# Gated linear attention in a hybrid trunk: the projections of a pair of heads traced ahead of the mixing of the pair before

## The chip, the cores and the metric

The kernel runs on one core of one Trainium2 chip. A core has a matrix engine (TensorE, PE in the profile, with its weight loads shown as PEld), VectorE (DVE), ScalarE (ACT), GpSimd (POOL), and SyncE (SP), which here only issues DMAs. The engines run side by side; each takes its own instructions strictly in the order in which the program lists them, and they wait for one another through semaphores. The metric is the device time of the program in microseconds: the median of several runs. One further execution is taken with the profiler; the views quoted below come from that execution.

## The reference, cut to what matters

One layer of a decoder trunk on 512 tokens and 16 meta tokens, 2048 wide. The normalised input goes through one wide projection, whose columns feed three causal mixers on separate heads: a gated DeltaNet (6 heads), gated linear attention or GLA (5 heads) and a forgetting attention (5 heads). All are multiplied by SiLU gates and go through one output projection. The change is in GLA alone:

```python
def gla_chunked(q, k, v, log_g):
    """S_t = diag(alpha_t) S_{t-1} + k_t v_t^T ; o_t = q_t S_t.
    q, k, log_g [B,H,T,dk]; v [B,H,T,dv]. Returns [B,T,H,dv]."""
    ...
        attn = jnp.einsum('bhid,bhjd,bhijd->bhij', q_c, k_c, dec)
        o = jnp.einsum('bhid,bhdv->bhiv', qd, s) + jnp.einsum('bhij,bhjv->bhiv', attn, v_c)
        s = s * gl[..., :, None] + jnp.einsum('bhjd,bhjv->bhdv', kd, v_c)

    log_g = jax.nn.log_sigmoid(gl @ w_gk2.astype(f32) + b_gk.astype(f32)) / GLA_NORMALIZER
    o_gla = gla_chunked(to_heads(gq, GLA_HEADS) * GLA_DK ** -0.5, to_heads(gk, GLA_HEADS),
                        to_heads(gv, GLA_HEADS), to_heads(log_g, GLA_HEADS))
    o_gla = gated_head_norm(o_gla, gz, gla_norm_w.astype(f32))
```

## The kernel before, in words

**Stages.** The program works through: loading and splitting the input, the gates, DeltaNet in two groups of three heads (keys, values, queries, inverse, mixing), the SiLU gates of GLA, GLA itself, five forgetting heads, and the output projection. All of the input projection is done in blocks of 128 columns by one helper, `inproj` (line 188): each block loads its weights in two halves of 128 x 1024 through SP (L136), splits each half into a high and a low part (ACT at L144, DVE at L145), and issues matmuls at L174: for each of 16 slices of the inner dimension three products (high by high, high by low, low by high), in one part of 512 columns (48 matmuls) or in two of 264 (96 matmuls, where the meta tokens are needed as well). The results stay in PSUM tiles of tag "b" (four buffers) until DVE takes them out, scaled (L285 and L287, helper `evac`).

**GLA.** The five heads go in pairs, p = 0, 1, 2 (the last pair is a single head). For each pair, one function does two things. The first is *projection*: keys gk and queries gq (for the last pair one block holds both), one block of values gv for each head, transposed on PE into token order (`tok_values`, L640 and L643, with copies by ACT at L641 and L644), and the gates: a small matmul (L669, tile pgk), bias (L671), a log-sigmoid on DVE and ACT (L672 to L675), and a running sum (L676), which gives gc. The second is *mixing*, from line 677 on: score matmuls at L717 (tiles pss) in eight levels, for blocks of 64, 32, 16, 8, 4, 2, 1 and the diagonal. For each level DVE and ACT prepare scaled keys and queries (L695 to L703) in two shared sets of tiles (kq), and DVE takes the scores out, by copies (L721, L725) or masked copies (L729). Then come the decayed keys (L736 to L743, with gkd and its transpose pkd), the meta part (L745 to L762), the states (L768, L770), the outputs (L777, L783), the head norm (L789 to L794), a transpose back (L797, tile pgt) and the product with the SiLU gate (L799).

**What sets the order.** The program is not written as one list per engine. A planner takes the instructions with their dependencies and lays out each engine's list when the program is built: of the instructions that it holds to be ready by its own timing, it takes the one with the lowest number of priority. That number counts up by one with each instruction in the order in which the Python code creates them. `tc.high_priority(offset=n)` makes the numbers of the instructions within it lower by n; after the block, the count goes on from where it stood ahead of the block. The split of the weights (lines 142 to 145) uses an offset of 1,000,000, so it is always taken first. Tiles are named by tag, and each tag has a fixed number of buffers: "m" (PSUM, 4) for everything on PE that is not a projection, "b" (PSUM, 4) for projections, "six" (8), "row" (7), "t15" (6), and a few small ones. An instruction that writes a new tile needs a free buffer of its tag.

**Names in the two parts.** Projection: gqk (keys, queries and gc; "six"), gvt (values; "six"), gvm ("t15"), vg, gu and gt ("row"), pvg, pwg and pgk ("m"). Mixing: gdd (tag "gd", 2), a (one buffer, scores of the fine levels), at (shared by all pairs, within the kq tiles), gkd, kdt and gqd ("row"), pss, pkd, pgm, pg0, pgn, pgo and pgt ("m"). Forgetting heads: fqk and fc ("six"), vf ("row"), pvf and others ("m").

Of the kernel before, what the change touches and what calls it, by code (L numbers as in the profile page):

```python
# [77 lines left out]
def tile_hybrid_trunk(ctx, tc, xT, xtok, mtok, w_gate, w_in, w_out, consts, lmask, fin_w, out, dbg=None):  # L78
# [14 lines left out]
    def row(name, dt=F32):  # L93
        return wk.tile([P, 3 + T], dt, tag="row", bufs=7, name=name)

    def t15(name, shape=(P, H, P), dt=F32):
        return wk.tile(list(shape), dt, tag="t15", bufs=6, name=name)
# [547 lines left out]

    kts, qts, ats = [], [], []

    def gla_pair(p):
        R = P if p < 2 else 64
        ne = 2 if p < 2 else 1  # L650
        qk = six.tile([P, 3, T], F32, tag="six", name=f"gqk{p}")
        kT, qT, gc = qk[:R, 0], qk[:R, 1], qk[:R, 2]
# [7 lines left out]
        vt = six.tile([P, 2, S], F32, tag="six", name=f"gvt{p}")  # L660
        vm = t15(f"gvm{p}", (NM, 2, P))
# [12 lines left out]
        A.activation(t, t, AF.Ln, bias=1.0)  # L674
        V.scalar_tensor_tensor(out=u, in0=u, scalar=0.0, in1=t, op0=ALU.min, op1=ALU.subtract)  # L675
        V.tensor_tensor_scan(gc, gsc[:R], u, 0.0, ALU.mult, ALU.add)  # L676
        SC = 1.0 / 16.0
        k4, q4, g4 = (a[:, NM:].rearrange("p (b t) -> p b t", b=NB) for a in (kT, qT, gc))
        n_n = ne * NB
# [4 lines left out]
        def scores(s, li):  # L684
# [11 lines left out]
            if s > 1:  # L696
                V.tensor_tensor(out=dv[:, :, 0, :], in0=ref, in1=gv[:, :, 0, :], op=ALU.subtract)
                A.activation(d, d, AF.Exp, scale=SC)
                V.tensor_tensor(out=kxv[:, :, 0, :], in0=kv[:, :, 0, :], in1=dv[:, :, 0, :], op=ALU.mult)
            else:  # L700
                A.activation(dv[:, :, 1, :], dv[:, :, 1, :], AF.Exp, scale=SC)
                kx = kT[:, NM:]
# [33 lines left out]
        V.tensor_tensor(out=d4, in0=g4[:, :, P - 1 : P].to_broadcast([R, NB, P]), in1=g4, op=ALU.subtract)  # L736
        A.activation(dd, dd, AF.Exp, scale=SC)
        G.tensor_tensor(out=d4, in0=d4, in1=k4, op=ALU.mult)
# [6 lines left out]
        V.tensor_tensor(out=dm, in0=gc[:, NM - 1 : NM].to_broadcast([R, NM]), in1=gc[:, :NM], op=ALU.subtract)  # L745
        A.activation(dm, dm, AF.Exp, scale=SC)
        V.tensor_tensor(out=dm, in0=dm, in1=kT[:, :NM], op=ALU.mult)
# [4 lines left out]
        qd = row(f"gqd{p}")[:, :S][:R]  # L752
        A.activation(qd, gc[:, NM:], AF.Exp, scale=SC)
        G.tensor_tensor(out=qd, in0=qd, in1=qT[:, NM:], op=ALU.mult)
        eg = wk.tile([P, NB], F32, tag="geg", name=f"geg{p}")[:R]
        A.activation(eg, g4[:, :, P - 1], AF.Exp, scale=SC)
        p0 = psm.tile([P, 512], F32, tag="m", name=f"pg0{p}")
# [127 lines left out]
    for g in range(2):  # L885
        for h in range(max(NF, H * g), H * g + H):
            gate_z("dz", h)
        st = dn_keys(g)
# [11 lines left out]
    kts += [kq[0][:, :S], kq[0][:, S : 2 * S]]  # L900
    qts += [kq[0][:, 2 * S :], kq[1][:, :S]]
    ats.append(kq[1][:, S:].rearrange("p (n t) -> p n t", t=P))
    for p in range(3):
        gla_pair(p)
    for h in range(GLA_HEADS):
        dump(f"ogl{h}", zs["gz", h])
    for h in range(FOX_HEADS):
# [176 lines left out]
```

## Time and profile before

| what | us |
|---|---|
| median of 3 runs | 1032.09 |
| lowest and highest run | 1031.01, 1033.81 |
| profiled execution, whole | 1035.39 |
| profiled execution, span from the first to the last instruction | 1033.7 |
| PE busy in the span | 1011.4 |
| weight loads busy (overlap PE) | 910.3 |
| DVE busy | 566.7 |
| ACT busy | 411.7 |
| POOL busy | 136.4 |

The mean granted TensorE clock of the profiled execution is 0.992 of full speed.

How to read the views: a row of a stretch gives its start and end, its length, and for each engine the busy time and the number of instructions, then the granted clock of PE and the share and rate of the DMAs. A row of the timeline gives the start, the duration, the engine, the line, the operation, the tile written and the tiles read (numbers left out), the count of merged instructions, and in brackets the idle time of the engine ahead of it and what ended it. A row of the waits gives who waited for whom, the total, how often, and the longest. Matmuls overlap in the pipeline, so that the duration of one is longer than the distance to the next.

### The profile page before, as it was taken

The page shows a single profiled execution, that of the slowest core. Times are in us where ns is not written, and L with a number is a line of the kernel's source. Part 1 is how long each engine was busy: PE and PEld are TensorE (multiplying, and loading weights), DVE is VectorE, ACT ScalarE, POOL GpSimd, SP SyncE. Part 2 cuts the span into 40 slices and gives each one's busy share as a digit, 9 for nine tenths or more (in the row PEclk, how much of TensorE's full clock was granted, in tenths as well). Part 3 has the DMA queues.
Part 4 walks back from the last instruction along what each step waited for, and adds up shares of the span by engine and source line. Part 5 has one row for each costly group of instructions (what it writes and reads, how often), then busy time and mean ns, then how long its engine had stood idle before and what let it go on. Part 6 is the DMA issues. An engine that isn't in the chain of part 4 may idle for free.

```text
span 1033.7 us, 19032 instructions
## 1 busy us (share of the span) xinstructions
PE 1011.4 (98%) x7799; PEld 910.3 (88%) x7799; DVE 566.7 (55%) x1240; ACT 411.7 (40%) x899; POOL 136.4 (13%) x137
## 2 busy tenths in 40 slices
PE   9999999999999998999989999999999999999996
PEld 7899999989999888899989879898998988888885
DVE  6366868856577883243747474445454574423234
ACT  6644533343455343243444444343333353213223
POOL 0022212221122222100101010110101010000014
PEclk9999999999999998999999999999999999999998
DMA  9613232323222233132112122222232254222244
GB/s 354 239 62 115 83 90 91 102 78 108 78 83 81 78 102 99 49 94 74 62 48 83 44 92 66 91 82 92 82 93 82 93 193 133 82 100 85 102 142 163
DMA packets 42347, 105.15 MB, mean 102 GB/s; under 512 B 10589, under 2 KB 13917, under 8 KB 42260
## 3 DMA queue, kind: packets, MB, share of 16 engines
q1 hardware_dynamic: 28000, 92.33, 26.3%
q10 hardware_dynamic: 14260, 11.61, 4.1%
q8 instruction: 61, 1.00, 0.4%
q14 instruction: 26, 0.21, 0.1%
HBM read 98.74 MB, written 5.05 MB: 100 GB/s over the span
## 4 chain that ended last, share of the span: by engine, by line
PE 66%; DVE 5%; DMA 3%; issue 3%; ACT 2%; POOL 1%; ACTq 0%; POOLq 0%; DVEq 0%
PE pp L174 39%; PE pa L932 15%; DMA sc<-ab 1%; PE pss L717 1%; POOL stgz L294 1%; DVE wlo L145 1%; PE pfo L877 1%; PE pfa L845 1%; PE py L593 1%; PE pb L932 1%; PE pfx L860 1%; DVE ab L465 1%; PE po L608 1%; PE po L607 1%; PE pa L570 0%
## 5 line engine op out<-in xcount | busy, mean ns | idle before, releaser
L174 PE MATMUL pp<-xh,whi 128*128 128x264 f32 (+2 forms) x1456 | 378.2, 311 | 0.8 <-DVE vg L285 0.5
L174 PE MATMUL pp<-xl,whi 128*128 128x264 f32 (+2 forms) x1456 | 378.2, 311 | 0.0
L174 PE MATMUL pp<-xh,wlo 128*128 128x264 f32 (+2 forms) x1456 | 376.5, 310 | 0.0
L174 PEld LDWEIGHTS pp<-xh,whi 128*128 128x128 f32 x1456 | 244.4, 189 | 16.8 <-issue 3.1
L174 PEld LDWEIGHTS pp<-xl,whi 128*128 128x128 f32 x1456 | 245.6, 190 | 14.0 <-issue 1.0
L174 PEld LDWEIGHTS pp<-xh,wlo 128*128 128x128 f32 x1456 | 245.2, 190 | 13.1 <-issue 0.2
L145 DVE TENSOR_TENSOR wlo<-raw,whi 128x1024 fp32r<-128x1024 f32 x110 | 137.1, 1246 | 112.0 <-ACT whi L144 110.4
L144 ACT CAST whi<-raw 128x1024 fp32r<-128x1024 f32 x110 | 115.4, 1049 | 202.3 <-PE pp L174 175.3
L932 PE MATMUL pa<-wloo,oh 128*128 128x512 f32 x224 | 88.0, 393 | 0.0
L932 PE MATMUL pa<-whio,ol 128*128 128x512 f32 x224 | 87.9, 393 | 0.0
L932 PE MATMUL pa<-whio,oh 128*128 128x512 f32 x224 | 78.3, 396 | 0.0
L145 DVE TENSOR_TENSOR wloo<-rawo,whio 128x1024 fp32r<-128x1024 f32 x29 | 35.8, 1236 | 76.4 <-ACT whio L144 76.3
L144 ACT CAST whio<-rawo 128x1024 fp32r<-128x1024 f32 x29 | 30.4, 1049 | 83.8 <-PE pa L932 56.8
L932 PEld LDWEIGHTS pa<-whio,ol 128*128 128x128 f32 x224 | 42.2, 188 | 9.7
L932 PEld LDWEIGHTS pa<-wloo,oh 128*128 128x128 f32 x224 | 42.1, 188 | 9.4
L932 PEld LDWEIGHTS pa<-whio,oh 128*128 128x128 f32 x224 | 41.9, 188 | 9.2
L294 POOL TENSOR_SCALAR stc<-cv 128x528 f32<-128x528 f32 (+1 forms) x18 | 28.1, 1562 | 164.5 <-DVE cv L368 164.5
L368 DVE SCALAR_TENSOR_TENSOR cv<-pb,cpk,cv 128x528 f32<-128x528 f32 (+1 forms) x54 | 40.8, 756 | 0.8
L959 POOL TENSOR_TENSOR acc<-acc,fw 128x512 f32<-128x512 f32 x12 | 15.7, 1348 | 158.6 <-DMA fw<-in_fin_w 158.6
L285 DVE TENSOR_TENSOR pb<-pp,rstd 128x264 f32<-128x264 f32 (+1 forms) x36 | 13.8, 423 | 16.0 <-PE pp L174 15.9
L465 DVE TENSOR_TENSOR ab<-ab,ot 51x30 f32<-51x30 f32 (+14 forms) x60 | 21.4, 357 | 1.4
L463 DVE TENSOR_TENSOR ot<-ab 51x30 f32<-51x30 f32 (+14 forms) x60 | 20.1, 334 | 3.1 <-DMA ab<-scmeta 1.5
(384 smaller groups left out, 1279.8 us busy)
## 6 DMA issues: line engine op xcount, KB each, us to landing
raw<-in_w_in SPq DMA_DIRECT2D x110, 512.0 KB, 3.3
rawo<-in_w_out SPq DMA_DIRECT2D x29, 512.0 KB, 3.3
xt<-in_xtok SPq DMA_DIRECT2D x8, 512.0 KB, 9.9
acc<-in_xtok ACTq DMA_DIRECT2D x16, 256.0 KB, 5.2
out<-acc SPq DMA_DIRECT2D x16, 256.0 KB, 3.0
xs<-in_xT SPq DMA_DIRECT2D x7, 528.0 KB, 6.5
gb<-gd ACTq DMA_DIRECT2D x2, 792.0 KB, 7.4
eg<-gd ACTq DMA_DIRECT2D x8, 192.0 KB, 3.7
```

Source lines behind the costliest of these rows:

```text
L144: A.copy(hi, raw)
L145: V.tensor_tensor(out=lo, in0=raw, in1=hi.bitcast(F32), op=ALU.subtract)
L174: mm = PE.matmul(p_[:, :nt], wt[:, j * m : (j + 1) * m], xx[k][:, t0 : t0 + nt], start=(k == 0 and wt is hi and xx is xh), stop=(k == KT - ...
L285: V.tensor_tensor(out=o, in0=p_[rows], in1=rstd[rows, t0 : t0 + n], op=ALU.mult)
L294: G.tensor_scalar_max(t, src, LOW)
L368: V.scalar_tensor_tensor(out=c, in0=pb[:, t0 + w : w + T], scalar=cwc[:, blk, w : w + 1], in1=c, op0=ALU.mult, op1=ALU.add)
L463: V.tensor_tensor(out=t3, in0=a3[:, j + 1 :, j : j + 1].to_broadcast([NN * 4 + H, m, j]), in1=a3[:, j : j + 1, 0:j].to_broadcast([NN * 4 + ...
L465: V.tensor_tensor(out=a3[:, j + 1 :, 0:j], in0=a3[:, j + 1 :, 0:j], in1=t3, op=ALU.add)
L593: PE.matmul(py[:, j * P : (j + 1) * P], uf[:, b * H + j, :], z[:, j, :], start=True, stop=True)
L607: PE.matmul(pj, at[:, b * H + j, :], y[:, j, :], start=True, stop=False)
L932: PE.matmul(p_, o_[:, s], w_, start=(first and n == 0), stop=(last and n == 2), **kw)
L959: G.tensor_tensor(out=acc[tb, cc], in0=acc[tb, cc], in1=fw[cc], op=ALU.mult)
```

## The change

The function for a pair is cut in two at line 677: `gla_project(p)` holds the projection, the value transposes and the gates, and returns its tiles; `gla_mix(p, st)` holds the rest, unchanged. The calls are then put in another order: projection 0, projection 1, mixing 0, projection 2, mixing 1, mixing 2, where mixings 0 and 1 are created with priority numbers lower by 500. The instructions themselves, their sizes and their tiles are the same.

```diff
@@ -645,7 +645,7 @@
     kts, qts, ats = [], [], []
 
-    def gla_pair(p):
+    def gla_project(p):
         R = P if p < 2 else 64
         ne = 2 if p < 2 else 1
         qk = six.tile([P, 3, T], F32, tag="six", name=f"gqk{p}")
...
         V.tensor_tensor_scan(gc, gsc[:R], u, 0.0, ALU.mult, ALU.add)
+        return R, ne, kT, qT, gc, qk, vt, vm
+
+    def gla_mix(p, st):
+        R, ne, kT, qT, gc, qk, vt, vm = st
         SC = 1.0 / 16.0
...
-    for p in range(3):
-        gla_pair(p)
+    gla = {0: gla_project(0), 1: gla_project(1)}
+    with tc.high_priority(offset=500):
+        gla_mix(0, gla[0])
+    gla[2] = gla_project(2)
+    with tc.high_priority(offset=500):
+        gla_mix(1, gla[1])
+    gla_mix(2, gla[2])
     for h in range(GLA_HEADS):
```

## The prediction

> **What bounds the kernel now.** First the page's busy times, then the same by stretches, to see where TensorE (PE) stands idle; the columns after each stretch are busy microseconds and instruction counts of PE, weight loads, VectorE (DVE), ScalarE (ACT) and GpSimd (POOL).
>
> ```profile
> PE 1011.4 (98%) x7799; PEld 910.3 (88%) x7799; DVE 566.7 (55%) x1240; ACT 411.7 (40%) x899; POOL 136.4 (13%) x137
> ```
>
> ```profile
> 0.00:50.00 50.00, 48.32 (x209) 39.18 (x210) 25.42 (x41) 34.51 (x59) 1.85 (x16) 1.00 0.80 296
> 200.00:250.00 50.00, 47.58 (x521) 45.88 (x521) 30.37 (x58) 18.65 (x31) 9.26 (x10) 0.97 0.30 93
> 400.00:450.00 50.00, 46.98 (x465) 42.80 (x464) 15.61 (x34) 18.27 (x43) 5.33 (x6) 0.93 0.25 76
> 499.00:549.00 50.00, 46.82 (x776) 44.38 (x776) 30.84 (x71) 21.86 (x57) 4.53 (x3) 1.00 0.19 61
> 549.00:558.00 9.00, 9.00 (x67) 7.95 (x66) 4.99 (x7) 2.50 (x4) 0.00 (x0) 1.00 0.24 67
> 558.00:598.00 40.00, 37.59 (x704) 35.55 (x704) 22.79 (x60) 18.17 (x51) 5.04 (x3) 1.00 0.18 62
> 598.00:610.00 12.00, 12.00 (x53) 8.79 (x51) 7.26 (x11) 3.27 (x7) 0.63 (x1) 1.00 0.33 101
> 610.00:646.00 36.00, 35.50 (x428) 31.25 (x427) 22.02 (x50) 15.54 (x37) 5.08 (x3) 1.00 0.20 65
> 646.00:1000.00 354.00, 353.68 (x1921) 304.32 (x1920) 158.71 (x338) 118.90 (x215) 18.82 (x28) 1.00 0.31 103
> 1000.00:1034.00 34.00, 25.40 (x125) 21.09 (x123) 12.60 (x21) 11.45 (x28) 15.69 (x12) 0.91 0.47 157
> ```
>
> PE is idle for 1033.7 − 1011.4 = 22.3 us of the whole span. Most of it lies at the start, in the two DeltaNet inverses (200 to 250, 400 to 450) and in the tail after 1000, none of which the change touches. GLA runs from 499 to 646: 499 to 549 is the mixing of pair 0, 549 to 558 the gates of pair 1, 558 to 598 the mixing of pair 1, 598 to 610 the gates of pair 2, 610 to 646 the mixing of pair 2. PE idles there for 3.18 + 0 + 2.41 + 0 + 0.50 = 6.1 us. That is the most that any order of the same instructions can give back on PE, but for a few tenths hidden in pipelined matmuls. Note the two gate stretches: the mixing stands still in them, and yet PE is busy for 9.00 of 9.00 and 12.00 of 12.00 us, with projections traced later. The waits of PE in and around GLA say what the 6.1 us are:
>
> ```profile
> PE pss L717 <- issue: 3.5, 3, 1.4
> PE pkd L742 <- DVE a L729: 1.1, 1, 1.1
> PE pp L174 <- DVE vg L285: 0.5, 2, 0.3
> PE pg L760 <- ACT gkm L751: 0.5, 1, 0.5
> PE pss L717 <- DVE kq L703: 0.5, 1, 0.5
> ```
>
> "issue" means that nothing in the profile was waited for. All three of these waits cut runs of two score levels (64 short matmuls each) issued back to back, as here:
>
> ```profile
> 520.30 0.76 PE L717 MATMUL pss<-kq 64*32 64x32 f32 x64
> 520.91 0.70 PE L717 MATMUL pss<-kq,kq 64*32 64x32 f32 x59
> 522.96 0.26 PE L717 MATMUL pss<-kq,kq 64*32 64x32 f32 x5 [1.35 <-issue]
> ```
>
> **The change, part by part.**
>
> Work: no instruction, byte or tile is added or removed. The sum is made of order alone: PE's 1011.4 us stay, and only its idle time can move.
>
> The numbers of priority. Counted in the code, a projection of a full pair is 374 instructions, its mixing 346. Before, the order is projection 0 (0 to 374), mixing 0 (374 to 720), projection 1 (from 720). After, projection 1 has 374 to 748, and mixing 0 is traced at 748 but ranks 500 earlier, 248 to 594. So mixing 0 ranks ahead of nearly all of the values and of the gates of pair 1, as before; only gk1, gq1 and the loads and first matmuls of gv2 come to rank ahead of its later levels. Those have run by then anyway (gv2 starts at 491.80, below). Mixing 1 ranks 467 to 813, projection 2 from 748: the same picture. By priority alone hardly anything moves.
>
> What does move is the handing out of tiles. The trace shows that tiles of one tag are given out in the order in which the program creates them, not to whoever is ready:
>
> ```profile
> 508.39 2.93 POOL L738 TENSOR_TENSOR gkd<-gkd,gqk 128x512 f32<-128x512 f32 x1 [30.79 <-ACT gkd L737]
> 527.09 0.63 PE L742 MATMUL pkd<-ident,gkd 128*128 128x128 f32 x4
> 527.56 1.44 DVE L285 TENSOR_TENSOR vg<-pp,rstd 128x264 f32<-128x264 f32 x4
> 549.29 0.71 PE L669 MATMUL pgk<-misc,cpk 16*128 16x264 f32 x2
> 550.04 0.49 DVE L671 TENSOR_SCALAR gu<-pgk,cpk 128x264 f32<-128x264 f32 x1 [0.88 <-PE pgk L669]
> ```
>
> gkd is ready at 508.39 + 2.93 = 511.3, but its transpose into a PSUM tile (tag "m", four buffers) runs at 527.09, behind all scores. The gate matmul pgk of pair 1 needs only misc and a constant, there since long before, and runs at 549.29, when the last "m" tile of mixing 0 has been handed out. After the change the "m" tiles of projection 1 (value transposes, gates) are created before the scores of mixing 0, so these scores must wait for them, whatever their priority.
>
> First scores. They run now at 510.60. The 192 matmuls of gv2 and gv3 start at 491.80, one every 0.12 us:
>
> ```profile
> 491.80 0.28 PE L174 MATMUL pp<-xh,whi 128*128 128x264 f32 x1
> 491.92 0.28 PE L174 MATMUL pp<-xl,whi 128*128 128x264 f32 x1
> 510.60 0.68 PE L717 MATMUL pss<-kq 64*64 64x64 f32 x16
> ```
>
> 192 × 0.12 = 23 us, with some 2 us of other PE work between: done at about 517, transposes and gates by 519. So mixing 0 starts its scores some 9 us later, with the operands of its first two levels long prepared. PE loses nothing: in those 9 us it runs gv3 and then gk2, and gk2 has PSUM, since the values of gv2 are now evacuated at once and not at 527.56.
>
> Gates. Each is a chain on DVE and ACT, for pair 1 from 549.29 to 556.80 + 1.26 = 558.1:
>
> ```profile
> 552.87 0.71 DVE L672 SCALAR_TENSOR_TENSOR gt<-gu 128x528 f32<-128x528 f32 x1
> 556.80 1.26 DVE L676 TENSOR_TENSOR_SCAN gqk<-gsc,gu 128x528 f32<-128x528 bf16 x1
> ```
>
> After the change the gates run under the mixing of the pair before, so the chain of mixings loses about 9 + 12 us of standing still, gives up 9 us at its start, and should end near 625 to 635 and not at 646. On PE this is worth 0, because PE idles 0.00 us in both stretches. What covers it is the stock of projections (gk2, gv4, fk, fv, fq, fz of forget head 0). Were that cover gone, up to 21 us would show. It isn't consumed faster: the shorter GLA needs less of it.
>
> DVE in mixing 0. It gains the gates (two L671 of 0.49, two of 0.71, the scan 1.26: 3.7 us) and the four vg evacuations (1.44 us), 5.1 us in a stretch where it is busy 30.84 of 50. Behind a DVE instruction in the planned order stand the masked copies L729, which free the score tiles, and so PE's next scores. Bounds: 0 (room of 19 us) to 5.1 us (each of them stops PE). I take 1.0, near the lower end: PE's waits for DVE in GLA (0.5 + 1.1 + 0.5) are small beside DVE's 88 us there (the five stretches).
>
> Waits for issue, 3.5 us. Bounds: all go (−3.5) or as many come again (+3.5: pairs of levels in mixing 2, which has none now). With gk2 in stock and DVE slower per level, the levels of mixing 0 should stand more apart; I take one wait of 1.35 away. The wait for kq (0.5) goes too, as those operands are early. The wait of pkd for L729 stays, and what is late next is the same copy.
>
> The Trainium skill ("Runtime: NRT & Kernel Launch", section on instruction fetch) says that crossing an instruction block costs little because the next one is fetched while the current one runs. The issue waits inside unbroken runs of scores, 3.5 us here, do not agree if they are such crossings; by the rule there would be nothing to win there, and the sum below would be −0.5 + 1.0 = +0.5 us.
>
> Switches. PE goes from projections to scores and back at some dozen places; a few more or fewer, at the tenth of a microsecond that a projection needs more than its 0.12 there, is ±0.5; I take 0.
>
> DMAs. The weight loads on SP keep their order. The one DMA of GLA on ACT's queue (the query rows of pair 2) is issued some 15 us earlier, inside mixing 0, where ACT is busy 21.86 of 50; what stands behind it is ACT's exponentials. Between 0 and a few tenths; 0 taken.
>
> Sum: −1.35 − 0.5 + 1.0 = −0.9, about −1 us. The profiled execution took 1035.4 us, 1.7 more than its span of 1033.7 and 3.3 more than the median of the runs, 1032.1. It would take 1034.4, the runs 1031.1.
>
> **The rivals.**
>
> Likeliest, PE-bound as before: the chain of mixings gets shorter, PE doesn't notice. For it: 353.68 of 354 us busy after 646, and the two gate stretches full. 1031.1, by itself between 1029 and 1034.
>
> The change does nothing at all: rank and hand-out undo each other, and even the chain keeps its length. Then 1032.1. Against it speaks pgk, which is held by tiles alone. It falls within the same class of result.
>
> Faster: the stock of projections between the levels grows so much that PE's waits in mixings 0 and 1 go: 3.5 + 1.1 + 0.5 + 0.5 = 5.6, so 1026.5. For it: projections wait for evacuated values (vg, 0.5), and after the change these are evacuated earlier. Against it: pairs of levels come from DVE's order in one mixing, which is kept.
>
> A part of the faster side, at 2 in 100: GLA is bounded by its chain, not by PE, and the 21 us come off: 1011. It needs a PE that could have done more in 549 to 558.
>
> The Trainium skill ("Perfetto Trace Analysis", section on the most-contended engine) says that matmul busy time flatters and weight-load busy time should be read. Loads are busy 910.3 us, 88%, and by that rule GLA has room of 147 − 127.9 = 19 us. The trace disagrees here: in 646 to 1000 loads are busy 304 of 354 with matmuls of 512 columns end to end.
>
> Slower: DVE becomes the pace of mixing 0. The scores wait for gv3 and the gates, then everything comes at once: six masked levels, gates of pair 1, six evacuations of pair 2. PE executes in order, so a score that was planned for a free DVE holds the projections behind it. The price is the 5.1 us of DVE above with little else gained, and it decides from about 3 us of such waits: 1032.1 + 5.1 − 0.5 = 1036.7. For it: 30.84 + 5.1 of 50 on DVE, and the wait for L729 shows that PE does stand behind it. Against it: the plan knows of DVE's work.
>
> **How the numbers follow.** 0.38 for PE-bound or no effect, 0.30 for faster (with the chain-bound 0.02), 0.32 for slower. A measurement of this kernel tells 0.3%, 3.1 us, from no change (its runs span 2.8 us), so the classes are the same three. The predicted time is the likeliest case's, 1031.1. The range: down to the waits all gone, 1026.5; up to DVE's whole 5.1 us plus part of the issue waits come again, 1038. About 2 in 10 are left out.
>
> **What would show it.** Right: pgk of pair 1 near 519 and not 549; first scores near 519; vg of pair 1 evacuated in two parts before 519; gates of pair 2 before mixing 1 ends; the last GLA transpose near 630; PE idle in GLA between 3 and 8 us; after 646 PE full. Wrong: pgk still after mixing 0 (tiles do follow priority); PE waits for L703 or L729 of more than 3 us in mixing 0; PE short of projections before the mixing of pair 2 ends; a later stage that changes by more than 2 us.

## The result, and the profile after

The changed kernel takes 1035.97 us (median of 14 runs, 1033.31 to 1039.63) against 1033.20 us for the kernel before on the same chip (14 runs). The ratio is 1.0027, with a 95% interval of 1.0015 to 1.0038: slower by about 2.8 us, or 0.27%. The time lies inside the predicted range, but the forecast was a gain of 1 us, and the interval excludes that. Run once more beside other kernels, the ratio was 1.0023 (1.0007 to 1.0039).

In the page of the kernel after, TensorE (PE) is busy 2.0 us longer than before, with the same 7799 matmuls. The second line is the queue that brings the instructions: packets, megabytes, share.

```profile
PE 1013.4 (98%) x7799; PEld 912.5 (88%) x7799; DVE 565.3 (55%) x1240; ACT 411.1 (40%) x899; POOL 131.2 (13%) x137
...
q8 instruction: 61, 1.00, 0.4%
```

The stretches of the kernel after (columns as in the prediction): scores of pair 0, rest of its mixing, scores of pair 1, rest of its mixing, and everything behind GLA.

```profile
524.00:545.00 21.00, 18.84 (x520) 17.56 (x520) 19.03 (x50) 7.43 (x13) 1.54 (x1) 0.92 0.20 59
545.00:570.00 25.00, 25.00 (x241) 23.62 (x228) 9.15 (x17) 12.67 (x43) 1.61 (x2) 1.00 0.20 65
570.00:592.00 22.00, 18.84 (x525) 17.04 (x523) 20.27 (x53) 7.81 (x13) 2.20 (x2) 0.99 0.19 63
592.00:616.00 24.00, 23.88 (x145) 20.13 (x146) 7.49 (x12) 12.13 (x41) 2.89 (x3) 0.94 0.14 45
647.00:1000.00 353.00, 353.00 (x1922) 304.02 (x1921) 158.62 (x337) 117.80 (x214) 19.11 (x28) 1.00 0.32 102
```

The column with 0.92 and 0.94 is the granted clock of PE. It was 1.00 in all of GLA before. Behind GLA hardly anything differs: from the end of the stage counted below to the last instruction it is 342.6 us before and 342.5 us after. The waits of PE in GLA have become two, both for "issue":

```profile
PE pss L721 <- issue: 3.1, 1, 3.1
PE pp L174 <- issue: 1.9, 1, 1.9
```

The timeline of PE shows them, the gate matmuls and first scores that the prediction speaks of, and the projections after the first wait. (Lines from the mixing on are four higher than before: L717 is now L721, L729 is L733, L742 is L746.)

```profile
520.71 0.71 PE L669 MATMUL pgk<-misc,cpk 16*128 16x264 f32 x2
524.37 0.69 PE L721 MATMUL pss<-kq 64*64 64x64 f32 x16
...
538.89 0.39 PE L174 MATMUL pp<-xl,whi 128*128 128x264 f32 x1 [1.90 <-issue]
539.11 0.41 PE L174 MATMUL pp<-xh,wlo 128*128 128x264 f32 x2
539.36 0.41 PE L174 MATMUL pp<-xh,whi 128*128 128x264 f32 x2
...
541.14 0.65 PE L174 MATMUL pp<-xh,whi 128*128 128x264 f32 x2
541.58 0.65 PE L174 MATMUL pp<-xl,whi 128*128 128x264 f32 x2
...
592.12 0.32 PE L721 MATMUL pss<-gqk 64*32 64x32 f32 x5 [3.05 <-issue]
```

Pairs of projection matmuls start 0.25 us apart at 539 and 0.44 us apart at 541: PE is "busy" in both, and its granted clock is 0.50 in the second (the rows under "When the clock is halved"). That is where the time went. To count it, I take the stage from the first gate matmul of pair 0 (L669) to the second forgetting head's first decay matmul (pfd, L850 after). It holds the same 2291 matmuls in all kernels of this study and takes 193.05 us before and 195.38 us after. Idle time of PE (no matmul running, summed over the stage) goes from 6.40 to 5.44 us, so 0.96 less. But 6.34 us of busy time after lie in half clock, and none before: half of that, 3.17 us, is counted as lost. −0.96 + 3.17 leaves 0.1 of the 2.33 us. (Projection matmuls of 264 columns start 0.22 us apart at half clock and 0.12 us apart at full clock, so that half is slightly too much; by these two numbers the loss is 2.8 us and 0.5 us are left.) The spans of the two profiled executions, 1033.7 and 1035.0 us, differ by 1.3 us only: ahead of the stage, where the change does nothing, the kernel after was 1.0 us quicker. The half clock in the DeltaNet inverses comes and goes there from execution to execution: at 403 us it lasted 6.83 us in the kernel before, 0 in the kernel after and 6.83 in the kernel after run again (experiment 8).

### The profile page after: what moved, and what is told of

It is laid out like the page before. It is cut to its first block, busy times and chain, and to the rows that moved or that the text cites. A ratio compares the mean times of both kernels' runs of the same rounds, so it can differ in the third digit from the quotient of the medians.

```text
span 1035.0 us, 19021 instructions
## 1 busy us (share of the span) xinstructions
PE 1013.4 (98%) x7799; PEld 912.5 (88%) x7799; DVE 565.3 (55%) x1240; ACT 411.1 (40%) x899; POOL 131.2 (13%) x137
## 4 chain that ended last, share of the span: by engine, by line
PE 53%; DVE 1%; issue 1%; ACT 1%; ACTq 0%; DVEq 0%
PE pp L174 29%; PE pa L941 15%; PE pss L721 1%; PE pfo L881 1%; PE pfa L849 1%; PE pb L941 1%; PE pfx L864 1%; PE pfd L850 0%; PE pgo L781 0%; PE pgk L669 0%; PE pfo L884 0%; PE pgo L787 0%; ACT sqf L965 0%; DVE acc L1034 0%; PE pgn L772 0%
## 5 line engine op out<-in xcount | busy, mean ns | idle before, releaser
L174 PEld LDWEIGHTS pp<-xh,whi 128*128 128x128 f32 x1456 | 244.0, 190 | 14.5 <-issue 0.9
```

Source lines behind the costliest of these rows:

```text
L174: mm = PE.matmul(p_[:, :nt], wt[:, j * m : (j + 1) * m], xx[k][:, t0 : t0 + nt], start=(k == 0 and wt is hi and xx is xh), stop=(k == KT - ...
```

## The experiments

Two things had to be explained: why PE stops for "issue", and when the clock is halved. The first theory, T1, was that both together are the loss: PE's instructions arrive in blocks, PE stops at a block's end when the next block is late, and behind a long stop the clock is halved. The rival, T2, was that the new order itself costs the time. The account of all kernels comes first, since every section below uses it. "Rest" is the stage less the idle time, less half of the busy time in half clock; all columns in us but the ratio and the windows.

| kernel | ratio to before (95%) | stage | idle | of it for issue | half-clock windows | rest |
|---|---|---|---|---|---|---|
| before | 1 | 193.05 | 6.40 | 3.5 | 0 | 186.65 |
| after | 1.0027 (1.0015 to 1.0038) | 195.38 | 5.44 | 5.0 | 2 | 186.78 |
| 1 after, shift 160 at the start | 0.9991 (0.9980 to 1.0002) | 193.27 | 4.89 | 0 | 1 | 186.67 |
| 2 after, shift 224 at the start | 1.0065 (1.0047 to 1.0082) | 195.91 | 6.52 | 2.9 | 2 | 186.49 |
| 3 before, shift 240 at the start | 1.0071 (1.0053 to 1.0090) | 195.07 | 7.02 | 4.3 | 1 | 186.34 |
| 4 after, no priority | 1.0016 (1.0002 to 1.0030) | 192.94 | 5.18 | 4.3 | 1 | 186.07 |
| 5 after, shift 160 in a wait | 1.0001 (0.9987 to 1.0016) | 193.27 | 4.94 | 0 | 1 | 186.64 |
| 6 before, shift 80 in a wait | 0.9982 (0.9968 to 0.9995) | 190.54 | 3.74 | 0.5 | 0 | 186.81 |
| 7 before, shift 240 in a wait | 1.0011 (0.9999 to 1.0023) | 194.30 | 5.81 | 3.1 | 1 | 186.78 |
| 8 after again | 1.0023 (1.0007 to 1.0039) | 196.10 | 4.99 | 4.6 | 3 | 186.58 |
| 9 as 5, lighter gates | 0.9957 (0.9944 to 0.9971) | 188.34 | 2.61 | 0 | 0 | 185.73 |
| 10 as 6, lighter gates | 0.9944 (0.9924 to 0.9965) | 187.47 | 1.68 | 1.2 | 0 | 185.79 |
| 11 after, lighter gates | 0.9979 (0.9968 to 0.9989) | 189.62 | 3.59 | 2.0 | 0 | 186.03 |
| 12 before, lighter gates | 0.9986 (0.9974 to 0.9997) | 189.39 | 3.38 | 2.9 | 0 | 186.01 |

In the ten runs with the same work (rows before to 8) the rest is 186.07 to 186.81, while the stage runs from 190.54 to 196.10. So idle time and half clock account for the stage to within 0.7 us, whatever the order.

**Where PE stops.** I numbered PE's records (matmuls, weight loads, semaphore instructions) from the start. The stops for "issue" of over 0.75 us in GLA, in both kernels and experiments 1 to 8 (1, 5 and 6 have none), are at

```
before:     8385, 8641, 9665
after:      8641, 10433
2 (+224):   9153
3 (+240):   8897, 10177
4:          8641, 10433
7 (+240):   8641, 8897, 10433
8:          8641, 10433
```

and every one of these numbers is 193 more than a multiple of 256. The instruction queue moved 61 packets and 1.00 MB, 16 KB each; PE's 15,685 records are 61.3 times 256. So PE stops at the end of a block of 256 instructions whose successor has not come. In the kernel after, PE entered the block ahead of the second stop at 587.08; the next block's packet began at 589.35 and took 1.19 us, and PE went on at 592.12. The same holds for every stop at a block end in the fourteen traces: PE goes on 1.2 to 1.6 us after the end of a packet of this queue. How fast PE uses up the block ahead decides most of it. In GLA 23 blocks lasted under 3 us, and 22 of them ended in a stop, of 0.4 to 3.05 us. Of 21 blocks of 3.4 to 4.1 us two did, where the next packet began only 3.8 and 4.0 us after PE had entered the block; of the slower blocks, none. Why a packet begins early or late, the traces do not show. The mean block lasts 17 us (1035 us by 61). Two levels of scores are 256 instructions and run in about 1.4 us, so a stop needs a block that lies mostly in scores. To move the block ends, experiments 1 to 3 add idle instructions at the start. In 1 and 2 the order of GLA on PE and DVE stays what it was; in 3 the planner moved a few of PE's instructions of GLA by some places.

### 1, 2, 3: block ends moved from the start

```diff
-    for i in range(10):
-        PE.matmul(pw[:, :P], ones, ones, start=True, stop=True)
+    for n in [P] * 10 + [32] * 40:
+        PE.matmul(pw[:n, :n], ones[:n, :n], ones[:n, :n], start=True, stop=True)
```

(56 instead of 40 in the second; 60, in the kernel before, in the third. Each is four instructions.)

> The kernel after, with 40 tiny 32x32 warm-up matmuls added at the very start (their sum is used by nothing), so that every later TensorE instruction sits 160 places further on in its 256-instruction blocks; the order inside the GLA stage stays that of the kernel after. Theory T1 (the loss is TensorE waiting for the next block of instructions inside the dense bursts of score matmuls, and the halved clock behind the long ones): the two waits of 1.9 and 3.0 us at the scores are gone or under 0.5 us together, the granted clock is 1.00 in the whole of the GLA stage, and that stage (first gate matmul of pair 1 to second fox matmul) shrinks from 195.4 us to about 188 us; the whole time falls by 5 to 7 us to about 1029, below the kernel before by 2 to 5. Theory T2 (the loss comes from the new order: the gates of pair 1 ahead of the scores, a later chain of mixings): the stage stays at 195 us and the time at that of the kernel after, 2 to 3 us over the kernel before.

> The kernel after with 56 such tiny matmuls, a shift of 224 places: another shift at which the count of block times puts no block end into a burst of scores. T1: as with 160, no long wait in GLA, clock 1.00, stage about 188 us, whole time 5 to 7 us under the kernel after. T2: no change against the kernel after.

> The kernel before with 60 tiny warm-up matmuls, a shift of 240 places that puts more block ends into its bursts of scores. T1: the waits for instructions in GLA grow from 3.5 us to about 5 us, at least one of them over 1.5 us with a halved clock behind it, so the stage grows from 193.1 to 195-198 us and the time is 2 to 5 us over the kernel before, though the order of its GLA stage is that of the kernel before. T2: the time of the kernel before.

The first went T1's way, by less than it said: no stop for issue is left, the stage is 2.1 us shorter than that of the kernel after. Its ratio of 0.9991 (0.9980 to 1.0002) lies clear of the 1.0027 (1.0015 to 1.0038) of the kernel after, and the order in GLA is the same: the loss goes when the block ends move. But the stage is 193.3 us and not 188, because other waits came in their place (below, at 5). The third went T1's way in the stage: 2.0 us longer, with a stop that halved the clock. The second is a miss of my count of block times: a stop of 2.9 us at another block end, 548.45, so the stage did not shrink.

The whole times of 2 and 3 say little, for a reason that I had not foreseen: their stage begins 3.6 and 2.2 us later than in the kernels without the shift. Here are two stretches at the start of the third, while it runs the small matmuls and behind them:

```profile
5.38:8.79 3.41, 3.41 (x104) 3.29 (x103) 1.91 (x3) 1.35 (x2) 0.00 (x0) 1.00 0.99 342
8.79:15.62 6.83, 6.83 (x38) 5.57 (x36) 4.91 (x9) 5.75 (x10) 0.00 (x0) 0.50 1.04 402
```

A stretch filled with 32x32 matmuls was followed by two windows of half clock. It looks as if small matmuls count as little or no work for the clock; no run varied their size alone. Experiments 5 to 7 therefore put the extra instructions elsewhere.

### When the clock is halved

The clock's records have one form in all traces, but for the last one at the kernel's end: stretches of 3.413 us, or of twice that, at half speed. In the kernel after they begin at 540.43 and 591.63, which are 51.20 = 15 x 3.413 us apart; in the kernel before at 232.73 and 403.40, 50 x 3.413 apart. So there is a fixed grid. The windows of that grid ahead of, and in, the half clock, first in the kernel after:

```profile
537.02:540.43 3.41, 1.54 (x12) 1.54 (x13) 3.31 (x8) 1.13 (x2) 0.00 (x0) 1.00 0.18 38
540.43:543.85 3.42, 3.42 (x17) 3.24 (x15) 2.63 (x9) 0.63 (x1) 0.00 (x0) 0.50 0.51 160
588.22:591.63 3.41, 0.85 (x90) 0.74 (x82) 2.58 (x9) 1.26 (x2) 0.00 (x0) 1.00 0.27 103
591.63:595.05 3.42, 2.93 (x18) 2.79 (x19) 1.78 (x5) 1.52 (x3) 0.32 (x1) 0.50 0.02 5
```

The three emptiest windows of the kernel before in GLA, none followed by half clock:

```profile
519.45:522.86 3.41, 2.16 (x131) 1.90 (x129) 1.77 (x6) 0.44 (x1) 0.00 (x0) 1.00 0.13 48
567.24:570.65 3.41, 2.27 (x135) 1.91 (x133) 3.38 (x9) 1.76 (x3) 0.00 (x0) 1.00 0.03 7
577.48:580.89 3.41, 2.15 (x103) 1.75 (x102) 2.70 (x7) 1.30 (x3) 0.00 (x0) 1.00 0.19 46
```

And the kernel without priority, experiment 4, whose two stops, of 1.7 and 2.6 us, are at the same two instructions as those of the kernel after:

```profile
536.08:539.50 3.42, 1.76 (x130) 1.55 (x130) 3.35 (x11) 1.90 (x3) 0.00 (x0) 1.00 0.08 28
539.50:542.91 3.41, 3.38 (x16) 3.38 (x16) 3.36 (x9) 0.00 (x0) 0.00 (x0) 0.50 0.52 142
587.28:590.69 3.41, 2.03 (x131) 1.77 (x129) 2.62 (x10) 0.63 (x1) 0.00 (x0) 1.00 0.50 159
590.69:594.10 3.41, 2.15 (x21) 2.09 (x22) 2.98 (x10) 1.90 (x5) 0.07 (x1) 1.00 0.02 5
```

And a window of experiment 7 with a stop of 1.5 us, and the one behind it:

```profile
523.66:527.07 3.41, 1.59 (x55) 1.18 (x43) 2.85 (x8) 0.69 (x3) 0.00 (x0) 1.00 0.29 101
527.07:530.48 3.41, 3.41 (x17) 3.41 (x17) 0.63 (x2) 2.30 (x6) 1.27 (x2) 0.50 0.15 58
```

Windows with PE busy 0.25, 0.45, 0.47 or 0.51 of the time are followed by half clock; those with 0.59, 0.63 or 0.67 are not. Over the traces of experiments 1 to 8 and both kernels, the fullest full-clock window in GLA that led to half clock was 0.54 busy, the emptiest that did not was 0.55. Outside of GLA the border is not as sharp: in the second DeltaNet inverse of experiment 7, among 32x32 matmuls, a window of 0.80 was followed by half clock (400.78), and in the first inverse of experiment 2 one of 0.53 was not (233.97). In experiment 4 the stop of 2.6 us at 589 to 592 fell across a border of the grid, 0.59 on one side and 0.63 on the other, and cost no clock at all. So a stop of 1.5 us or more can cost a further 1.7 us, by the chance of the grid, and the stops of 1.0 to 1.35 us of the kernel before did not. The Trainium skill ("TensorE: Matmul & The Clock Gate", section "What's actually happening") says that the window is 3413 ns long and doesn't start with the kernel; the traces agree. Its rule in the section "HAM oscillation", no idle gaps of PE above about 3.4 us, does not hold as a bound here: a stop of 1.90 us led to half clock.

### 4: trace order alone; and priority alone

```diff
-    with tc.high_priority(offset=500):
-        gla_mix(0, gla[0])
+    gla_mix(0, gla[0])
...
-    with tc.high_priority(offset=500):
-        gla_mix(1, gla[1])
+    gla_mix(1, gla[1])
```

> The kernel after without the two higher priorities: the new order of the trace alone. The order on TensorE differs from the kernel after only in where some late matmuls of the mixings stand. T1: scores keep their places in their blocks up to a few instructions, so the same one or two long waits, and a time within 2 us of the kernel after. T2 (the higher priority is what hurts): back to the kernel before, about 2.8 us less. If the higher priority helps, then slower than the kernel after by the longer chain of mixings, 0 to 3 us.

The stops are at the same two instructions (1.7 and 2.6 us), and the ratio of 1.0016 has an interval that overlaps that of the kernel after. So the stops come with the trace order alone, and the priorities are not needed for them. How much of the loss does is less clear: the lower end of the interval, 1.0002, hardly excludes the kernel before, and the profiled stage, with one half window, is 192.94 us, no longer than in the kernel before. The other half, the old order with the two priorities, changes nothing: the planner then gives every engine the very same list as in the kernel before. The prediction's count of ranks, "by priority alone hardly anything moves", holds.

### 5, 6, 7, 8: block ends moved at no cost

In the kernel after PE waits 2.5 us at 402 to 405 us, in the second DeltaNet inverse, for line 485's operands (3.0 us in the kernel before). There the extra matmuls cost little or nothing; they write what the real ones then overwrite.

```diff
-        for n in range(NN):
+        for n in range(NN + 20 * g):
             for q in range(2):
                 lo_, hi_ = ...
-                mm = PE.matmul(pm[lo_, n, :], an[hi_, n, lo_], uc[hi_, n, :], start=True, stop=True)
-                if n + q == 0:
-                    behind(mm, PM[g])
+                e = n - 20 * g; m = e % NN
+                mm = PE.matmul(pm[lo_, m, :], an[hi_, m, lo_],
+                               (uc if e >= 0 else an[:, :, :32])[hi_, m, :], start=True, stop=True)
+                if e + q <= 0:
+                    behind(mm, PM[g] + 7 * g)
```

(20 gives a shift of 160; 10 and 30, in the kernel before, give 80 and 240. In 5 the order of GLA is the same on every engine as in the kernel after. In 6 and 7 the planner also moved a few instructions of GLA by some places.)

> The kernel after with 40 extra 32x32 matmuls (overwritten by the real ones) put into the 2.5 us wait of TensorE at 402 to 405 us, where they cost nothing: every instruction of the GLA stage stands 160 places further on in its 256-instruction block, and the order of that stage is unchanged. Theory T1 (block ends inside the bursts of scores make TensorE wait, and a wait that leaves a 3.413 us window of the clock's grid less than half busy costs a further window at half clock, 1.7 us): no wait for instructions in the stage, at most one half window, stage 191.5 to 193.5 us instead of 195.4, whole time 2 to 4 us under the kernel after, that is at or just below the kernel before. Theory T2 (the new order costs the time by itself): stage 195 us, time of the kernel after.

> The kernel before with 20 such extra matmuls in the same wait, a shift of 80 places. T1: the waits for instructions in GLA fall from 3.5 us to about 1.2 us, none long enough for a half-clock window; stage 190.5 to 192 us instead of 193.1 unless another wait takes their place; whole time 1 to 2.5 us under the kernel before. T2: no change.

> The kernel before with 60 such extra matmuls in the same wait, a shift of 240 places: block ends fall worse, as in the earlier run with the same shift made at the start of the kernel, but without the half-clock windows that it had at its start. T1: waits for instructions of 4 us in GLA, one of them about 2 us with a half window behind it, stage about 195 us, whole time 1.5 to 3 us over the kernel before. T2: no change.

> The kernel after once more, unchanged, so that its clock grid falls at another place against its instructions. T1: the waits for instructions stay at the same two instructions with about the same length (1.9 and 3.0 us); the longer one leaves a window under half busy in nearly every phase, the shorter one only in some, so one or two half windows; stage = 186.5 us + idle time + half of the half-clock time within 0.4 us, so 193.5 to 195.5. T2: a stage of 195.4 us whatever the clock does.

The sixth is within T1's numbers: stops for issue 0.5 us, no half clock, stage 190.54, and a kernel that beats both, at 0.9982. The seventh is slower in the stage by 1.3 us where T1 said 2, and its ratio of 1.0011 cannot be told from 1. The intervals of 6 and 7 do not overlap. So the old order, but for a few moved instructions, gives 190.5, 193.1 or 194.3 us in the stage according to where its block ends fall; the waits for issue (0.5, 3.5 and 3.1 us) and the half window of the last make up most of the difference. The eighth repeats the two stops with 1.6 and 3.0 us, and this time three half windows (two of them behind the longer stop: the first of these, at 591.38, was itself only 0.66 busy); the stage is 196.10, above what I had allowed, and the account holds (rest 186.58). Over the 12 runs of the eighth the mean granted clock is 0.9907, over the 35 runs of the kernel before beside it 0.9950. The loss in the clock is thus no accident of the profiled executions.

The fifth gives T1 and T2 each a part. No stop for issue is left, and its median is 2 us below that of the eighth beside it (1033.95 and 1035.89; the intervals of the two ratios overlap, so that by whole times the first experiment is the stronger proof). Yet it is only as fast as the kernel before, and its stage is 2.7 us longer than that of the sixth. Its waits of PE, first, and then those of the sixth:

```profile
PE pkd L746 <- DVE a L733: 3.8, 2, 2.2
PE pss L721 <- DVE kq L707: 0.5, 1, 0.5
PE pss L721 <- DVE a L733: 0.4, 2, 0.2
```

```profile
PE pkd L742 <- DVE a L729: 1.4, 2, 0.9
PE pss L717 <- issue: 0.5, 1, 0.5
```

Where the stops go, VectorE (DVE) becomes what PE waits for, and the wait of 2.2 us brings the half window. The scores of pair 0 point to the reason; first in the fifth, then in the kernel before:

```profile
523.50:544.50 21.00, 18.59 (x534) 17.24 (x533) 19.35 (x51) 7.43 (x13) 1.54 (x1) 1.00 0.19 59
```

```profile
510.00:531.00 21.00, 17.82 (x528) 16.26 (x527) 15.09 (x42) 7.53 (x14) 1.80 (x3) 1.00 0.23 76
```

DVE is busy for 19.35 of 21 us in the new order, with the next pair's gates among its work, and for 15.09 in the old. The scores of pair 0, first to last, take 17.9 us in the fifth and 14.5 us in the sixth.

### 9, 10, 11, 12: less work on DVE in the gates

```diff
-        V.scalar_tensor_tensor(out=t, in0=u, scalar=-1.0, in1=u, op0=ALU.mult, op1=ALU.min)
-        A.activation(t, t, AF.Exp)
+        A.activation(t, u, AF.Exp, scale=-1.0)
         A.activation(t, t, AF.Ln, bias=1.0)
-        V.scalar_tensor_tensor(out=u, in0=u, scalar=0.0, in1=t, op0=ALU.min, op1=ALU.subtract)
-        V.tensor_tensor_scan(gc, gsc[:R], u, 0.0, ALU.mult, ALU.add)
+        V.tensor_tensor_scan(gc, gsc[:R], t, 0.0, ALU.mult, ALU.subtract)
```

The same function for arguments of ordinary size; what is left out is the guard against an overflow of exp(-u).

> The kernel of the fifth run (new order, block ends out of the bursts) with less VectorE work in the gates: the logarithm of the sigmoid is taken as minus ln(1 + exp(-u)) without the two instructions of 0.70 us that guard it against large negative arguments, 1.4 us of VectorE less per pair, at the place where the new order puts the gates of the next pair, in front of the mixing. Theory V (in the new order VectorE, which now does those gates while the scores wait for it, is late with the score tiles; this is what the two waits of pkd, 3.8 us together, and the half window behind the second are): these waits fall to 1.5 us or less together, no half window in the stage, stage 189.5 to 191.5 us instead of 193.3, whole time 1.5 to 3.5 us under the fifth run's. Theory L (pkd waits for the latency of the chain through ScalarE and TensorE, not for VectorE's load): pkd still waits 3 us or more, stage 193 us.

> The same lighter gates in the kernel of the sixth run (old order, block ends out of the bursts). Theory V: in the old order the gates of a pair stand between two mixings, where VectorE is not what TensorE waits for, so next to nothing is won: pkd waits 1.4 us as before, stage 190 to 191 us, time within 1 us of the sixth run's. Theory L: the same. If both orders gain alike, VectorE's load mattered in both and the order is not the reason for the 2.7 us between the fifth and the sixth run.

> The kernel after with the lighter gates and without the extra matmuls: the lighter gates alone. If the four stages add up as in the account stage = 186 us + idle time + half of the half-clock time, the block ends stay near the bursts (they move by a few places with the planner's order), so waits for instructions of 2 to 5 us and one or two half windows: stage 190 to 194 us, time between that of the kernel before and 4 us under it. If the extra matmuls did nothing for the ninth run, the stage is 188.3 us again.

> The kernel before with the lighter gates alone. By the account: waits for instructions of about 3.5 us as in the kernel before, no half window, 1 us less of other waits: stage 190 to 192 us, time 2 to 3.5 us under the kernel before. If the extra matmuls did nothing for the tenth run, the stage is 187.5 us again and the time 5.5 us under the kernel before.

Theory V was that DVE, which in the new order does the gates while the scores wait for it, is late with the score tiles. The ninth gained more than V said (stage 188.34; 0.9957 against 1.0001 for the fifth), though its waits of pkd fell to 2.0 and not to 1.5 us. No half window is left: its longest wait is 1.4 us.

```profile
PE pkd L746 <- DVE a L733: 2.0, 2, 1.4
PE pss L721 <- DVE kq L707: 0.6, 1, 0.6
```

But V also said that the old order would gain next to nothing, and that was wrong: the tenth gains 3.1 us in the stage over the sixth. Idle time falls by 2.3 us in the new order and by 2.1 in the old, and the rest by 0.9 and 1.0; what the new order gains beyond that is its half window, 1.7 us. As both gain, the new order is not shown to be slower by itself: of the 2.7 us between the fifth and the sixth, 1.7 are the half window and 1.2 idle time, and 0.9 us are left in the stage between 9 and 10. That DVE's load is what counts in both orders fits, but is not shown apart from the order of instructions: with the lighter gates the planner also put PE's instructions of GLA, some 150 to 200 of 3415, in other places. Why the rest falls by a microsecond, with the same matmuls, I have not found out. In 11 and 12, without the extra matmuls, stops for issue of 2.0 and 2.9 us in all are back, and the stage is 1.3 and 1.9 us longer than in 9 and 10. PE and DVE have the same lists of GLA in 11 as in 9, and in 12 as in 10, so this difference comes from the block ends alone. The whole time of the twelfth fell by 1.4 us by its ratio, less than the 2 to 3.5 expected, although its profiled stage is 3.7 us shorter than that of the kernel before; its 12 runs have a mean clock of 0.9937, the kernel before beside it 0.9947, so that other executions than the profiled one seem to have had half windows. The tenth is the fastest kernel of the study: 1028.39 us beside 1033.93, 0.9944; 9 and 10 can't be told apart by their intervals.

## Why the prediction was wrong

**The step that failed** is the first of the sum: "PE's 1011.4 us stay, and only its idle time can move." PE's busy time rose to 1013.4, because 6.34 us of matmuls ran at half clock. The clock was no term of the sum. It measured about +3 us (3.2 by the count above), more than any term that I took. The row for it was in the prediction's own fences: the stretches 200 to 250 and 400 to 450 show a clock of 0.97 and 0.93, where PE has its longest waits, and 1.00 in GLA, where no wait is over 1.4 us. I read these rows for idle time alone. (The base was off as well: 1032.1 us was the median of three runs, and fourteen give 1033.2.)

**Idle time**, the sum that I did make, came to −0.85 before rounding and was −0.96. That is luck in part, and so is that the measured time lies inside the range: its upper end was priced with waits for DVE and for issue, and not with the clock. "I take one wait of 1.35 away" had the wrong sign: the waits for issue went from 3.5 to 5.0 us, inside the bounds of ±3.5 that I gave. Waits for DVE went from 2.4 us or so to nothing that the waits list, where I had +1.0. They were hidden: with the same order and no stops for issue, in the first and fifth run, PE waits for DVE again.

**What the issue waits are** was left as a question, and with it the only way to size them. They are block ends. In the sentence on the Trainium skill ("Runtime: NRT & Kernel Launch", section "Instruction fetch mechanics"), crossing a block is mostly hidden. That is so for blocks that last longer than 4.1 us, none of which ended in a stop here, and not for bursts of scores, where one crossing cost up to 3.05 us.

**DVE as the pace of mixing 0**, the rival on the slow side, is borne out in the first and fifth run, where no stop covers it: PE waits 1.5 us in mixing 0 for the copy before pkd, of the 5.1 us that I had priced there, and 2.2 us in mixing 1, which I had not priced. In the changed kernel itself it does not show. My "room of 19 us" for DVE was the mean of a stretch of 50 us. In the 21 us of the scores, in the fifth run, there is room for 1.65.

**Tiles handed out in the order of creation** was right: pgk of pair 1 runs at 520.71 (I said 519, before 549.29), its values leave in two parts at 505.36 and 517.65, the gates of pair 2 come at 568 to 571, before mixing 1 ends at about 617, and behind 647 PE is full. First scores came at 524.37, 5 us later than I had counted.

**The chain of mixings** did not get shorter: the last transpose of GLA is at 646.68 (644.76 before), where I said 630. It starts 14 us later instead of 9, and its score stretches take 20.9 and 21.8 us instead of 16.5 and 15.1. Whether a shorter chain would be worth nothing on PE was therefore not put to the test; that PE is busy for 353.00 of 353 us behind GLA fits it.

## What to carry to other kernels

On a PE-bound kernel, "busy" is not work: read the granted clock beside it, by windows of the clock's own grid, and count a wait of 1.5 us or more at up to 1.7 us more than its length for each half window behind it. Bursts of very short matmuls use up blocks of 256 instructions faster than they arrive; where a change moves such bursts, the place of the block ends alone can cost or save as much as the change is worth (here up to 2.8 us of the stage for lists that were the same), so measure an order at two or three shifts before you judge it. Judge the load of an engine by the stretch in which it is needed and not by a mean over the stage.

## What the runs showed of the hardware

- PE stopped at block ends, 256 instructions apart, for 0.4 to 3.05 us, in 22 of the 23 cases in GLA where the block before was used up in under 3 us; it went on 1.2 to 1.6 us after the end of a packet of 16 KB, which took about 1 us. In the case of 3.05 us that packet began 2.3 us after PE had entered the block.
- A fixed grid of 3.413 us for PE's clock: a window with PE busy for less than about 0.54 of it was followed by one at half speed, in GLA; 0.55 and more was not.
- 32x32 matmuls seem to count as little work there: a window full of them (3.41 of 3.41 us) was followed by 6.83 us of half clock.
